# Eight of sixteen gates moved to the seven-product form, the filler's pace in the attention halved, and the first half of the heads' results fetched inside the last pair of heads

## The chip, the cores and the metric

The kernel runs on one core of one Trainium2 chip. The core has five engines that run their own instruction streams side by side: TensorE (PE, matmuls; PEld is its weight load), VectorE (DVE), ScalarE (ACT), GpSimd (POOL) and SyncE (SP, used here only to issue DMAs). An engine takes its instructions in the order in which they were put down when the program was built; where one waits on a semaphore, all behind it on that engine wait too. The metric is the device time of one execution in microseconds (us); lower is better. The reference time of the kernel before is the median of three runs.

## The reference

One decoder block on x of 1024 tokens by 1024 channels, float32, one layer. The part that matters here is the token mixer:

```python
proj = xn @ w_in                      # xn: RMSNorm(x); 1024 x 5136
(sb_q, sb_k, sb_v, g_q, g_k, g_v, g_r, g_a, gate_sb, gate_gla) = split(proj)
o_sb  = stick_breaking_attention(...) # 8 heads x 64, causal, blocks of 128
o_gla = gla_chunked(...)              # 4 heads, dk 64, dv 128
y = (sigmoid(gate_sb  + b_gate[0]) * (o_sb  @ w_branch_sb)
   + sigmoid(gate_gla + b_gate[1]) * (o_gla @ w_branch_gla))
h = x + y @ w_out
h = h + conv_ffn(rms_norm(h))         # gated MLP, d_ff 2816, causal conv of width 3
```

The two merge gates together are 2048 columns of `w_in`, that is 16 blocks of 128 channels; a "gate" below is one such block for all 1024 tokens. Gates 0 to 7 belong to the stick-breaking branch and 8 to 15 to the GLA branch.

## The kernel before, in words

All tensors stay float32 in effect: each operand is split into a high part (rounded to the matmul's float32 form) and the low remainder, and a product is three matmuls (high x high, high x low, low x high). `split` (L119, L110) does this with a cast on ACT and a subtraction on DVE; `add`, `sub`, `mul` (L116, L110, L113) are DVE operations; `mac` (L196) is the loop of matmuls, of 128x128 weights against 512 columns.

The stages in order of time:

1. **Norm and values** (0 to about 114 us): RMSNorm of x, transposes into four quarters `xq["11"]` to `xq["22"]` (token half, channel half), the value projections (L367), and the sums of quarters `s1` to `s4` for the seven-product form.
2. **Seven-product projections** (about 114 to 311 us), `fast` (called at L618): one job takes two blocks of 128 columns of `w_in` against all tokens. Written directly that is 2 blocks x 2 token halves x 8 channel blocks x 3 = 96 matmuls; with seven products of half-size operands in place of eight (Winograd's form of Strassen) it is 7 x 4 x 3 = 84, at the price of additions on DVE: four for the weights' sums, seven splits and seven to combine the products. `project_pairs` (L454) lists the jobs: two for the GLA queries and keys, four for the attention's queries and keys, two for the output gate `gr`, and `N_GATES`/2 = 2 for the first four merge gates. `keep` (L520) finishes a job: for a gate, a sigmoid of 128x1024 on ACT and a DMA to `gate_d` from ACT's queue.
3. **Attention** (about 311 to 540 us), `attend` (L705). Four pairs of heads (`j`); in each, four pairs of query blocks (`tp`); in each, both heads (`e`). A query block `i` sees `i+1` key blocks, in chunks of up to four blocks. For a chunk, `weigh` (L665) makes the logits (2 matmuls, L672), a sigmoid on ACT (L674) and a scan on DVE (L677, or L679 where a chunk goes on from another); `turn_weights` (L683) transposes the result block by block on PE (L686) and splits it; `gather` (L689) multiplies it with the values (L695), adds a bias on ACT (L701) and writes the head's result, as a high and a low part, to `osb_d` from SP's queue (L703). Up to six chunks, or twelve blocks, are under way between `weigh` and `turn_weights` (`AHEAD`, `BLOCKS`). Over all heads this is 8 x 36 = 288 blocks.
4. **Gates in between.** The other 12 gates are made directly by the generator `gates` (L539), 24 matmuls for each token half, cut in four steps of six. `attend` yields the number of blocks after each chunk, and the loop at L757 runs one gate step for each `FILL` = 3.6 blocks owed; six more steps come early (L742), and a sigmoid (L567) and a DMA follow every fourth step. Steps of the second token half need `xq["21"]`, which `whole21` (L605) fetches again from `x21_d` early in the attention and casts on ACT (L613). The first three gates do their second half last. What is left is run after the attention: four steps at L957, the rest at L969.
5. **Between attention and GLA** (about 540 to 565 us): loads for the GLA (L776 to L781), then the heads' results: for each token half `th` and each of four blocks `k`, two DMAs from `osb_d` (L964), one add and one split give `ob[th]`. Each DMA's target is a buffer of the pool `t2` (11 of them), each `ob[th]` takes two of the 16 buffers of pool `t8`.
6. **GLA with the first branch in between** (to about 620 us), then the second branch, the output projection, the FFN (L196 again as seven-product jobs, then L1155) and the final norm.

The order of instructions on each engine is set when the program is built, by a list scheduler that follows the order of the program's text as a priority; gate steps stand 25 places lower than their place in the text (`LATER`).

Of the kernel before, what the change touches and what calls it, by code (L numbers as in the profile page):

```python
# [17 lines left out]
P = 128  # L18
# [4 lines left out]
HALF = 512  # L23
SBH, SBD = 8, 64
# [10 lines left out]
C_GATE = 3088  # L35
T2 = 11
T4 = 14
FILL = 3.6
EACH = 0
LATER = 25  # L40
MORE = 1
# [11 lines left out]
GLA = 2, 3  # L53
PACES = 0, 0, 0, 1
EARLY = 6
N_GATES = 4
AT_END = 51
N_READY = 1
N_OPS = 11
# [6 lines left out]
def block_kernel(ctx: ExitStack, tc: tile.TileContext, x, norm_mix_g, w_in, b_gate, w_alpha_up, b_alpha,  # L66
                 gla_norm_g, w_branch_sb, w_branch_gla, w_out, norm_ffn_g, w_ffn_in, conv_w, conv_b,
                 w_ffn_out, norm_final_g, out):
    nc = tc.nc
# [7 lines left out]
    def nm(s):  # L77
        uid[0] += 1
        return f"{s}_{uid[0]}"
# [7 lines left out]
    def t8(dt=F32R):  # L87
        return sb.tile([P, 2 * D], dt, tag="t8", name=nm("t8"), bufs=16)

    def t4(dt=F32):  # L90
        return sb.tile([P, D], dt, tag="t4", name=nm("t4"), bufs=T4)

    def t2(dt=F32):
        return sb.tile([P, HALF], dt, tag="t2", name=nm("t2"), bufs=T2)

    def bank():
        return ps.tile([P, HALF], F32, tag="bank", name=nm("bank"), bufs=8)

    def dram(name, rows, cols):
        return dp.tile([rows, cols], F32, tag=name, name=name)  # L100

    def by(a, k):
        return a.rearrange("p (k c) -> p k c", k=k)

    def quarter():

        return [by(t8(), 4) for _ in range(2)]

    def sub(o, a, b):
        nc.vector.tensor_tensor(out=o, in0=a, in1=b, op=ALU.subtract)  # L110
# [4 lines left out]
    def add(o, a, b):  # L115
        nc.vector.tensor_tensor(out=o, in0=a, in1=b, op=ALU.add)  # L116

    def split(h, l, src):
        nc.scalar.copy(h, src)  # L119
        sub(l, src, h.bitcast(F32))  # L120
# [39 lines left out]
    osb_d = dram("osb_d", 2 * SBH * SBD, S)  # L160
# [4 lines left out]
    def fill(steps, n):  # L165
        for _ in range(n):
            next(steps, None)
# [286 lines left out]
    def project_pairs():  # L454
# [4 lines left out]
        for j in range(0, 4, 2):  # L459
            yield tuple((C_GR + n * P, gr_d, n * P) for n in (j, j + 1))  # L460
        for g in range(0, N_GATES, 2):
            yield tuple((C_GATE + n * P, gate_d, n * P) for n in (g, g + 1))
# [76 lines left out]
    def gates():  # L539
# [5 lines left out]

        gs = range(N_GATES, 2 * NK)
        order = [(g, (0,)) for g in gs[:N_HALVES]]
# [135 lines left out]
    def turn_weights(ke, nb, ah, al):  # L683
# [2 lines left out]
            nc.tensor.transpose(pt[:, b * P:(b + 1) * P], ke[:, b * P:(b + 1) * P], ident)  # L686
        split(ah, al, by(pt[:, 0:nb * P], nb))

    def gather(head, tp, ah, al):  # L689
        po = bank()  # L690
        nb = 2 * tp + 2
        for b in range(nb):
            c0 = 0 if b < nb - 1 else P
            for n, a in enumerate((ah, al)):
                nc.tensor.matmul(po[:, c0:2 * P], vt[b][:, head, :], a[b // 4][:, b % 4, c0:],  # L695
                                 start=(b == 0 and n == 0), stop=(b == nb - 1 and n == 1))
        o = t2()[:, 0:2 * P]
        for n in range(2):
            c = slice(n * P, (n + 1) * P)
            i = head * NT + 2 * tp + n  # L700
            nc.scalar.activation(o[:, c], po[:, c], AF.Identity, bias=vend[:, i:i + 1])  # L701
        for n, r in enumerate(HALVES):
            nc.sync.dma_start(osb_d[n * HALF + head * 64:n * HALF + (head + 1) * 64, tp * 2 * P:(tp + 1) * 2 * P], o[r])  # L703

    def attend():  # L705

# [42 lines left out]
        while todo:  # L749
            flush()  # L750
            while late:
                gather(*late.popleft())
            yield 2
# [3 lines left out]
    for w in attend():  # L757
        owed += w + EACH
        while owed >= FILL:
            owed -= FILL  # L760
            fill(gate_steps, 1)
# [11 lines left out]
    for p in range(2):  # L773
        rows = slice(p * P, (p + 1) * P)
        v, kt = by(t8(F32), 2), t4()
# [114 lines left out]
    def branch(b, o, w):  # L890

        def pieces(i):
            if i < NK:
                if i % 2 == 0:
                    raws.append(load(w[:, i * P:(i + 2) * P], 4))
                return piece(raws[-1][:, :, i % 2 * P:(i % 2 + 1) * P])

        raws = []
        nxt = pieces(0)
        yield  # L900
        for i in range(NK):
            wp, nxt = nxt, pieces(i + 1)
            for th in range(2):
                sg = t2()
                g = b * NK + i
                nc.sync.dma_start(sg, gate_d[g * P:(g + 1) * P, th * HALF:(th + 1) * HALF])
                if i % 4 == 0:
                    if b == 0:
                        yb[th, i // 4] = by(t8(F32), 4)
                    else:  # L910
                        yq[th, i // 4] = quarter()
                pt = bank()
                mac([a[:, 0:2] for a in wp], [a[:, 0:2] for a in o[th]], 2, pt, stop=False)
                yield
                mac([a[:, 2:4] for a in wp], [a[:, 2:4] for a in o[th]], 2, pt, start=False)
                y = yb[th, i // 4][:, i % 4]
                if b == 0:
                    mul(y, pt, sg)
                else:
                    mul(sg, pt, sg)  # L920
                    add(sg, sg, y)
                    split(*(a[:, i % 4] for a in yq[th, i // 4]), sg)
                yield
# [31 lines left out]
            fill(wsteps, paced[n] % PACES[n] == 0)  # L955

    fill(gate_steps, BEFORE)  # L957
    ob = []
    for th in range(2):
        ob.append(quarter())  # L960
        for k in range(4):
            halves = t2(), t2()
            for n, v in enumerate(halves):
                nc.sync.dma_start(v, osb_d[n * HALF + k * P:n * HALF + (k + 1) * P, th * HALF:(th + 1) * HALF])  # L964
            add(halves[0], *halves)
            split(*(a[:, k] for a in ob[th]), halves[0])
    first_branch = branch(0, ob, w_branch_sb)
    fill(first_branch, 1)
    fill(gate_steps, 128)  # L969
# [2 lines left out]
    n = 0  # L972
# [319 lines left out]
```

## Time and profile before

| | us |
|---|---|
| median of three runs | 1414.32 (1413.01 to 1415.31) |
| profiled execution, its own time | 1414.5 |
| its span in the trace | 1412.8 |
| PE busy | 1382.6 (98% of the span) |
| DVE busy | 1055.3 (75%) |
| ACT busy | 647.0 (46%) |
| POOL busy | 90.0 (6%) |

Busy time is the union of an engine's instructions in the trace. The end of a matmul is modelled and overlaps the next one's start, so "busy" on PE says that no gap was seen, not that matmuls followed each other at full rate; the rate is read from the distance between starts. The chain of waits names, for each piece of time, the work that the end of the execution hung on.

### The profile page before, as it was taken

Reading aid. Unit: us, or ns where it says so; the run is one execution under the profiler, and the core shown is the slowest. Engines: PE = TensorE matmul, PEld = TensorE weight load, DVE = VectorE, ACT = ScalarE, POOL = GpSimd, SP = SyncE. Lnnn points to the kernel's source line nnn. Section 1 sums busy time; section 2 is a strip of 40 time slices with the busy share of each in tenths; the row PEclk is TensorE's granted clock in tenths of the full one; section 3 lists DMA queues with packets and bytes.
Section 4 is the critical chain, followed back from the end, with each engine's and each line's share of the span. In section 5 each row is a group of like instructions: output and inputs, shape, how many; then the busy total and the mean of one; then the engine's idle time right before and its main releaser. Section 6 shows DMA issues by size and latency. Waiting matters only on the chain.

```text
span 1412.8 us, 18288 instructions
## 1 busy us (share of the span) xinstructions
PE 1382.6 (98%) x6577; PEld 1143.9 (81%) x6577; DVE 1055.3 (75%) x1618; ACT 647.0 (46%) x1246; POOL 90.0 (6%) x159
## 2 busy tenths in 40 slices
PE   7999999999999998999999999999999999999996
PEld 6788888887888887878888788888888888888885
DVE  6387776767887774738446988999888977896764
ACT  6234334647766563643234543333333334454653
POOL 0002122200000000300000000000000000000000
PEclk9999999999999999999999999999999999999999
DMA  6334345476644447465324434564554537953232
GB/s 249 129 109 137 108 153 186 137 207 197 164 117 112 124 157 252 170 226 176 120 90 134 111 98 149 188 208 146 175 179 149 171 106 269 324 159 99 98 110 90
DMA packets 163131, 221.84 MB, mean 157 GB/s; under 512 B 10729, under 2 KB 106027, under 8 KB 162528
## 3 DMA queue, kind: packets, MB, share of 16 engines
q1 hardware_dynamic: 142272, 157.56, 36.1%
q0 software_dynamic: 13472, 48.56, 9.2%
q10 hardware_dynamic: 7296, 14.55, 2.8%
q8 instruction: 52, 0.85, 0.2%
q14 instruction: 39, 0.32, 0.1%
HBM read 158.37 MB, written 62.26 MB: 156 GB/s over the span
## 4 chain that ended last, share of the span: by engine, by line
PE 92%; DVE 3%; DMA 2%; ACT 1%; issue 0%; SPq 0%; DVEq 0%; ACTq 0%
PE bank L196 56%; PE bank L1155 15%; PE bank L367 6%; PE bank L1022 5%; PE bank L695 2%; PE bank L672 2%; PE bank L686 2%; DVE t L110 2%; DMA t<-osb_d 1%; PE bank L320 1%; DMA t<-x_d 1%; DVE t L116 1%; PE bank L427 1%; PE bank L826 1%; ACT t L119 0%
## 5 line engine op out<-in xcount | busy, mean ns | idle before, releaser
L196 PE MATMUL bank<-t,t 128*128 128x512 f32 x3648 | 869.3, 394 | 5.7 <-DVE t L110 5.2
L196 PEld LDWEIGHTS bank<-t,t 128*128 128x128 f32 x3648 | 681.6, 188 | 153.2 <-DVE t L110 7.1
L110 DVE TENSOR_TENSOR t<-t,t 128x512 fp32r<-128x512 f32 (+2 forms) x651 | 432.0, 698 | 89.7 <-ACT t L119 82.7
L119 ACT CAST t<-t 128x512 fp32r<-128x512 f32 x537 | 311.3, 620 | 313.5 <-DVE t L110 68.7
L116 DVE TENSOR_TENSOR t<-bank,t 128x512 f32<-128x512 f32 x252 | 170.2, 686 | 99.3 <-PE bank L196 58.3
L1155 PE MATMUL bank<-t,t 128*128 128x512 f32 x924 | 209.6, 390 | 0.0
L1155 PEld LDWEIGHTS bank<-t,t 128*128 128x128 f32 x924 | 173.5, 188 | 36.0
L110 DVE TENSOR_TENSOR t<-bank,t 128x512 fp32r<-128x512 f32 (+4 forms) x128 | 72.3, 580 | 38.6 <-ACT t L119 37.8
L110 DVE TENSOR_TENSOR t<-t 128x512 f32<-128x512 f32 (+1 forms) x124 | 88.9, 725 | 6.2 <-DMA t<-in_w_ffn_in_dram 4.1
L367 PE MATMUL bank<-t,t 128*128 128x512 f32 x384 | 91.1, 396 | 0.0
L116 DVE TENSOR_TENSOR t<-t,t 128x512 f32<-128x512 f32 x115 | 75.7, 689 | 19.9 <-ACT t L486 15.6
L1022 PE MATMUL bank<-t,t 128*128 128x512 f32 x384 | 88.9, 391 | 0.0
L1053 ACT ACTIVATE t<-t,vcol 128x1024 f32<-128x1024 f32 x22 | 27.4, 1244 | 126.8 <-DVE t L116 126.8
L367 PEld LDWEIGHTS bank<-t,t 128*128 128x128 f32 x384 | 72.2, 190 | 15.4 <-DVE t L110 0.4
L1022 PEld LDWEIGHTS bank<-t,t 128*128 128x128 f32 x384 | 71.7, 188 | 14.6
L119 ACT CAST t<-bank 128x512 fp32r<-128x512 f32 (+3 forms) x124 | 61.7, 510 | 38.4 <-PE bank L320 19.2
L1055 DVE SCALAR_TENSOR_TENSOR t<-t,vcol,t 128x1023 f32<-128x1023 f32 (+1 forms) x44 | 56.3, 1279 | 14.1 <-ACT t L1053 13.9
L677 DVE TENSOR_TENSOR_SCAN t<-t,t 128x128 f32<-128x128 f32 (+1 forms) x64 | 51.6, 816 | 20.2 <-ACT t L674 19.8
L672 PE MATMUL bank<-t,t 128*128 128x128 f32 (+3 forms) x192 | 55.0, 366 | 0.3 <-DVE t L110 0.3
L686 PE MATMUL bank<-ident,t 128*128 128x128 f32 x288 | 53.9, 274 | 0.1
L674 ACT ACTIVATE t<-bank 128x128 f32<-128x128 f32 (+3 forms) x96 | 45.8, 502 | 7.1 <-PE bank L672 6.8
L679 DVE TENSOR_TENSOR_SCAN t<-t,t,zero 128x512 f32<-128x512 f32 x32 | 41.0, 1281 | 9.8 <-ACT t L674 8.8
(133 smaller groups left out, 743.9 us busy)
## 6 DMA issues: line engine op xcount, KB each, us to landing
t<-in_w_ffn_in_dram SPq DMA_DIRECT2D x50, 512.0 KB, 4.3
t<-in_w_in_dram SPq DMA_DIRECT2D x43, 512.0 KB, 5.3
act_d<-t POOLq DMA_DIRECT2D x22, 512.0 KB, 6.2
t<-in_w_ffn_out_dram SPq DMA_DIRECT2D x22, 512.0 KB, 5.8
wsum_d<-t POOLq DMA_DIRECT2D x22, 512.0 KB, 4.5
t<-act_d SPq DMA_DIRECT2D x22, 512.0 KB, 5.8
t<-wsum_d SPq DMA_DIRECT2D x44, 256.0 KB, 3.2
t<-sqk_d SPq DMA_DIRECT2D x40, 256.0 KB, 4.2
```

The costliest lines, as they stand in the source:

```text
L110: nc.vector.tensor_tensor(out=o, in0=a, in1=b, op=ALU.subtract)
L116: nc.vector.tensor_tensor(out=o, in0=a, in1=b, op=ALU.add)
L119: nc.scalar.copy(h, src)
L196: nc.tensor.matmul(pt, a[:, kk], b[:, kk], start=start and kk == 0 and m == 0, stop=stop and kk == k - 1 and m == 2)
L367: nc.tensor.matmul(pt, a[:, k % 4, t], b, start=k == 0 and m == 0, stop=k == NK - 1 and m == 2)
L672: nc.tensor.matmul(z[:, 0:w], q[:, a, e, ts_], kk[:, e, b0 * P:b1 * P], start=a == 0, stop=a == 1)
L674: nc.scalar.activation(ke[:, 0:w], z[:, 0:w], AF.Sigmoid, scale=-SBD ** -0.5)
L677: nc.vector.tensor_tensor_scan(out=kr, data0=kr, data1=above[:, 0:w], initial=1.0, op0=ALU.mult, op1=ALU.max)
L686: nc.tensor.transpose(pt[:, b * P:(b + 1) * P], ke[:, b * P:(b + 1) * P], ident)
L1022: nc.tensor.matmul(pt, a[:, k % 4, t], b, start=(k == 0 and m == 0), stop=(k == NK - 1 and m == 2))
L1055: nc.vector.scalar_tensor_tensor(out=cv[:, i:], in0=av[:, :S - i], scalar=col(V_CW, (2 - i) * NF + f), in1=cv[:, i:], op0=ALU.mult, op1=AL ...
L1155: nc.tensor.matmul(pts[m][i], a[:, t], b, start=(k == 0 and x_ == 0), stop=(k == NH - 1 and x_ == 2))
```

## The change

Three edits. `N_GATES` goes from 4 to 8, so that two more jobs of the seven-product stage make gates 4 to 7, and `gates` makes 8 gates (8 to 15) and not 12. `FILL` goes from 3.6 to 6, so that a gate step is run for every six blocks of the attention. And the fetch of the heads' results becomes a function that `gather` calls for the last head: after the second of its four pairs of query blocks for the first token half, after the fourth for the second half. In the text of the program the second call now stands ahead of the loads for the GLA; before, both halves came behind them.

```diff
-FILL = 3.6
+FILL = 6
-N_GATES = 4
+N_GATES = 8
+    ob = []
+
+    def fetch_heads(th):
+
+        ob.append(quarter())
+        for k in range(4):
+            halves = t2(), t2()
+            for n, v in enumerate(halves):
+                nc.sync.dma_start(v, osb_d[n * HALF + k * P:n * HALF + (k + 1) * P, th * HALF:(th + 1) * HALF])
+            add(halves[0], *halves)
+            split(*(a[:, k] for a in ob[th]), halves[0])
+
     def gather(head, tp, ah, al):
...
             nc.sync.dma_start(osb_d[n * HALF + head * 64:n * HALF + (head + 1) * 64, tp * 2 * P:(tp + 1) * 2 * P], o[r])
+        if head == SBH - 1 and tp % 2:
+            fetch_heads(tp // 2)
...
     fill(gate_steps, BEFORE)
-    ob = []
-    for th in range(2):
-        ob.append(quarter())
-        for k in range(4):
-            halves = t2(), t2()
-            for n, v in enumerate(halves):
-                nc.sync.dma_start(v, osb_d[n * HALF + k * P:n * HALF + (k + 1) * P, th * HALF:(th + 1) * HALF])
-            add(halves[0], *halves)
-            split(*(a[:, k] for a in ob[th]), halves[0])
     first_branch = branch(0, ob, w_branch_sb)
```

## The prediction

> **What bounds the kernel now.** I read the page's chain first: its shares by engine, then by line.
>
> ```profile
> PE 92%; DVE 3%; DMA 2%; ACT 1%; issue 0%; SPq 0%; DVEq 0%; ACTq 0%
> ```
>
> The end hangs on TensorE for 92% of the span, so a matmul saved is worth its time wherever the other engines keep up, and a pause of PE costs its length. Next comes the chain in order of time, for the price of a matmul, and the windows (columns: window, its length, busy time and count on PE, PEld, DVE, ACT, POOL, granted clock, DMA share, GB/s; the second answer is L196 alone, PE and PEld).
>
> ```profile
> 253.41 38.31 PE bank L196 x168
> 292.15 19.09 PE bank L196 x84
> ```
>
> ```profile
> 253.40:293.20 39.80, 39.80 (x179) 32.97 (x179) 33.22 (x52) 26.01 (x38) 7.77 (x14) 1.00 0.48 150
> 758.00:797.00 39.00, 38.15 (x179) 30.76 (x178) 38.49 (x64) 25.38 (x48) 1.59 (x3) 1.00 0.57 162
> 797.00:1193.00 396.00, 396.00 (x1749) 328.01 (x1748) 344.78 (x500) 145.65 (x217) 22.85 (x43) 1.00 0.47 158
> ...
> 311.50:538.70 227.20, 225.60 (x1329) 194.04 (x1326) 170.03 (x240) 145.20 (x326) 0.00 (x0) 1.00 0.50 145
> ...
> 311.50:538.70 227.20, 146.56 (x525) 95.37 (x525) 1.00 0.50 145
> ```
>
> The first chain row is the eighth and ninth of the ten seven-product jobs, the ninth being the first of the two gate jobs; the second row is the last job, also gates. Two jobs of 84 matmuls take 38.31 us, 0.228 us a matmul, with no gap, while DVE is busy for 33.22 of 39.80 us. The attention runs from 311.5 to 538.7: 227.2 us, PE without gaps but for 1.6 us, DVE at 170.03/227.2 = 75%. Of its PE time the 525 matmuls of L196 take 525 x 0.228 = 119.7 us (all 12 gates are 12 x 48 = 576; 51 come later); the attention's own logits, transposes and gathers have the other 107.5 us. So here the direct gates are more than half of what PE does, and hide everything else.
>
> Then the joint of attention and GLA, by the timeline of PE (start, busy time; in brackets the idle time before and its releaser), the windows there, and the waits (total, times, longest).
>
> ```profile
> 552.86 1.97 PE L196 MATMUL bank<-t,t 128*128 128x512 f32 x7
> 556.45 0.96 PE L196 MATMUL bank<-t,t 128*128 128x512 f32 x3 [1.62 <-DVE t L110]
> ...
> 562.18 1.65 PE L196 MATMUL bank<-t,t 128*128 128x512 f32 x5 [2.78 <-DVE t L110]
> 564.23 3.54 PE L196 MATMUL bank<-t,t 128*128 128x512 f32 x9 [0.40 <-ACT t L119]
> ```
>
> ```profile
> 560.00:565.00 5.00, 2.42 (x7) 1.51 (x8) 4.10 (x8) 1.76 (x3) 0.40 (x1) 0.84 1.04 381
> 565.00:570.00 5.00, 5.00 (x30) 3.87 (x29) 4.68 (x13) 1.82 (x4) 2.03 (x6) 0.82 1.00 350
> ```
>
> ```profile
> DVE t L116 <- DMA t<-osb_d: 3.7, 2, 2.1
> ACT t L613 <- DMA t<-x_d: 2.8, 2, 1.9
> ```
>
> PE stands for 1.62 + 2.78 + 0.40 = 4.80 us: the first branch's matmuls wait for the split of the fetched heads' results (L110 and L119 behind the add L116). Then nine matmuls take 3.54 us where 9 x 0.228 = 2.05 would do, another 1.5, at a granted clock of 0.84 and 0.82. The joint costs 6.3 us.
>
> **The change part by part.**
>
> *Jobs added.* Two more jobs are 168 matmuls: **+38.3 us** by the row of x168. What they bring to the other engines is what the present gate jobs bring, and that row shows it hidden: DVE 33.22, ACT 26.01 of 39.80. Their weight loads on SP and gate DMAs on ACT's queue are those of jobs 9 and 10 again (DMA share 0.48). If that cover were gone PE would wait for DVE; at 83% it is far from it. Bounds: 38 to 39.
>
> *Direct gates removed.* Four gates are 4 x 48 = 192 matmuls, 192 x 0.228 = **-43.8 us**, all from the attention if the pacing lets go as many as the work shrinks. It does: 288 blocks / 3.6 = 80 steps before, 288 / 6 = 48 after, 32 fewer, and four gates are 32 steps (two halves of four). The remainder run after the attention stays about as it is (51 matmuls), and covers the joint as now. Both parts together are 24 matmuls less, -5.5 us. PE alone would then finish the attention in 227.2 - 43.8 = 183.4 us.
>
> *What is late next in the attention.* VectorE. Its 170.03 us do not shrink with the gates:
>
> ```profile
> L679 DVE TENSOR_TENSOR_SCAN t<-t,t,zero 128x512 f32<-128x512 f32 x32 | 41.0, 1281 | 9.8 <-ACT t L674 8.8
> L110 DVE TENSOR_TENSOR t<-bank,t 128x512 fp32r<-128x512 f32 x45 | 30.3, 674 | 1.8 <-ACT t L119 1.8
> L110 DVE TENSOR_TENSOR t<-t,t 128x512 fp32r<-128x512 f32 x34 | 21.8, 679 | 3.7 <-ACT t L119 3.6
> ```
>
> Scans and the splits of transposes belong to the blocks (groups of 312 to 530 us, columns: busy, mean ns, idle before). Only the split of gate weights goes: each of the 15 visits to a gate splits two halves of 128x512; eight gates have 11 visits, so 4 x 2 x 0.679 = 5.4 us go, and the moved fetch adds four adds and four subtractions, 8 x 0.68 = 5.4. DVE keeps 170 us, which in 183.4 is 93%, up from 75%. It cannot use all of it: at the start and the end it waits for work, whatever the fill.
>
> ```profile
> 313.49 1.25 DVE L677 TENSOR_TENSOR_SCAN t<-t,t 128x128 f32<-128x128 f32 x2 [1.32 <-ACT t L674]
> ...
> 319.82 1.29 DVE L110 TENSOR_TENSOR t<-t,t 128x512 fp32r<-128x512 f32 x2 [2.98 <-ACT t L119]
> ...
> 534.80 1.89 DVE L110 TENSOR_TENSOR t<-bank,t 128x512 fp32r<-128x512 f32 x3 [4.54 <-ACT t L119]
> ```
>
> That is 1.3 + 3.0 + 4.5 = 8.8 us, and 2 us more after its last piece at 536.7. 170 of 183.4 - 10.8 = 172.6 us is 98%. So PE and DVE become bounds together, which no row of the attention shows yet. Two rows bound it: 758 to 797 us has DVE at 38.49 of 39.00 with PE idle 0.85 us (2.2%, or 4 us in 183); 797 to 1193 us has DVE at 344.78/396 = 87% and PE without a gap. If the attention ran DVE at no more than those 87%, it would last 170 / 0.87 = 195.4 us, 12 above PE's own time. Bounds of this stall: 0 to 12; I take **+3**, near the first row, since the 758 to 797 us are the only ones that show both full. It should sit where the keys and queries of the next pair are split, where DVE already has most to do, against the next 20 us without them:
>
> ```profile
> 450.00:470.00 20.00, 20.00 (x116) 16.96 (x116) 17.47 (x24) 13.28 (x31) 0.00 (x0) 1.00 0.26 74
> 470.00:490.00 20.00, 20.00 (x126) 17.80 (x125) 13.73 (x20) 9.77 (x24) 0.00 (x0) 1.00 0.48 145
> ```
>
> In 20 x 183.4/227.2 = 16.1 us the first needs 17.5 us of DVE: some 1 us over, at each of three such places.
>
> *The start.* ACT waits 2.8 us in all for the reload of x's quarter (L613), with casts and sigmoids of the chunks queued behind it and DVE behind those; PE, full of gate steps, loses little:
>
> ```profile
> 346.45 0.39 PE L695 MATMUL bank<-t,t 128*128 128x256 f32 x1 [1.17 <-DVE t L110]
> ```
>
> With 0.6 of the gate steps PE has less to bridge it: between 0 and 2.8 us more; I take **+1**.
>
> *The fetch inside the last pair.* Eight loads of 256 KB on SP, four adds, four casts on ACT, four subtractions, at about five sixths of the attention. The adds wait for loads, and behind them on DVE are scans and splits; behind the loads on SP are the write-outs of other heads' results, gate weights and the GLA's loads. The present fetch made DVE wait 3.7 us (row above), among crowded DMAs. The pool `t2` is shared with the chunks, so the look-ahead shrinks while it runs. Bounds 0 to 4; I take **+1.5**.
>
> *The joint.* When the last results are written, only half the fetch is left, and the matmuls of the first token half no longer wait. DVE's timeline has the adds of the fetch, first and last:
>
> ```profile
> 548.22 0.69 DVE L116 TENSOR_TENSOR t<-t,t 128x512 f32<-128x512 f32 x1
> ...
> 562.85 0.67 DVE L116 TENSOR_TENSOR t<-t,t 128x512 f32<-128x512 f32 x1
> ```
>
> Both halves end with the split behind 562.85, when PE goes on for good; the first ends where PE goes on at 556.45. Half a fetch is thus done near 556.4, and PE, fed without a gap to 554.8 (row of 552.86) and then by matmuls of the first token half, has next to nothing to wait for. The 4.80 us of idle go, and with them the slow clock, 6.3 in all. Against it the GLA's loads now stand behind the second fetch in the text. I take **-5.3**, between 0 and -6.3.
>
> The Trainium skill, "TensorE: Matmul & The Clock Gate" (Part 1, The HAM clock gate), says that the array's clock falls to half after an idle window of about 3.4 us and is given back after a busy one of that length. The two rows at 560 to 570 us, 0.84 and 0.82 in the mean behind gaps of 1.62 and 2.78 us, agree with a clock lost for part of that time, though no single gap was that long. The rule speaks against thinner filling: gaps in the attention would cost more than their length (a rival below).
>
> **Sum.** +38.3 - 43.8 + 3 + 1 + 1.5 - 5.3 = -5.3 us. The profiled execution took 1414.5 us, its span 1412.8; 1414.5 - 5.3 = 1409.2, and since the median 1414.32 is 0.2 lower: **1409.0**.
>
> **The rivals.**
>
> *A, the forecast:* attention 186 to 191 us, joint mostly closed; 1406 to 1412. Chance 0.40.
>
> *B, all of it lands:* look-ahead of twelve blocks absorbs DVE's peaks, the stalls are nil: -5.5 - 6.3 = -11.8, 1402.5. For it: DVE's total still fits, 98% of what it can use. Against: only 39 us of trace show such packing. 0.15.
>
> ```profile
> L674 ACT ACTIVATE t<-bank 128x512 f32<-128x512 f32 x48 | 29.0, 606 | 6.7 <-PE bank L672 6.6
> L119 ACT CAST t<-bank 128x512 fp32r<-128x512 f32 x45 | 26.8, 597 | 10.0 <-PE bank L686 9.9
> ```
>
> *C, slower: VectorE's chain takes over the attention.* Scan, cast and split wait in turn, and PE, in order, stands at each transpose whose scan is late. It decides from a use of DVE below 87%: then the 195.4 us are past and the stall of 12 eats the whole 11.8. At 83%, what the gate jobs show beside a bound PE (33.22/39.80), it is 170/0.83 = 205 us, 21.4 over PE's time: 1414.3 + 21.4 - 11.8 = 1424. For it: twelve blocks of look-ahead are 227.2/288 x 12 = 9.5 us now and 7.6 after, against a chain of some 4.4 us (sigmoid 0.61 and cast 0.60 by the rows above, two scans of 1.28, split 0.67) plus transposes and queues. Against: DVE waits today mostly because nothing is there to do. 0.18.
>
> *D, the joint stays:* the early fetch finds no buffers (`t8` is nearly full: four quarters, the values and the last pair take 15 of 16) and is done late, or the GLA's loads now collide with it and PE waits for those. Then the 5.3 are not had: 1414.3. 0.20.
>
> *E, the clock:* gaps in the attention bring the slow clock. Ten us at 0.83 lose 1.7 us; at the start and the three crowded places that is 4 x 1.7 = 6.8 on top of the forecast: 1415.8. The skill's page on the clock gate, named above, would have it so for gaps beyond 3.4 us; the attention's rows now show 1.00 throughout. 0.07.
>
> **How the numbers follow.** Noise and small differences: 0.2% is 2.8 us, about what a measurement of this kernel tells from no change, so faster is below 1411.5 and slower above 1417.1. Faster: B 0.15, most of A 0.37, 0.03 of D: 0.55. Same: 0.03 of A, 0.15 of D, 0.03 of C, 0.04 of E: 0.25. Slower: 0.15 of C, 0.02 of D, 0.03 of E: 0.20. The range leaves out the lowest of B and the upper half of C: 1402 to 1420.
>
> **What would show it.** The seven-product stage ends near 311.5 + 38.3 = 349.8 us. The attention then lasts 186 to 191 us with DVE around 90%; B shows 183 and no gaps on PE, C 196 or more with PE idle before L686 and L695, released by DVE. At the joint the waits of PE for L110 are gone and the granted clock stays at 1.00; D shows gaps there of 4 us or more. Everything from the second branch on keeps its length. The forecast is wrong if the attention's gaps sum to over 9 us, or if the 38.3 us of the two jobs come with gaps of their own.

## The result and the profile after

The kernel after takes 1427.85 us (median of 5 runs, 1426.43 to 1429.32), the kernel before on the same chip 1414.41 (5 runs): a ratio of 1.0097 with a 95% interval of 1.0087 to 1.0108. It is **slower**, by about 13.4 us. The forecast was 1409.0, faster; the range ended at 1420. The profiled execution took 1427.94 us, 13.4 more than that of before, so it can be taken apart stage by stage.

Three marks cut the span: the first matmul of the attention (the small transposes of L651), the last bias of the attention on ACT (L701 before, L713 after), and the stretch of 250 matmuls of L196 in the chain of waits, from which on both kernels run alike.

| | attention starts | last bias | x250 starts | attention lasts | joint lasts |
|---|---|---|---|---|---|
| before | 311.18 | 538.88 | 620.32 | 227.7 | 81.4 |
| after | 349.11 | 543.40 | 633.58 | 194.3 | 90.2 |
| difference | +37.9 | +4.5 | +13.3 | -33.4 | +8.8 |

(The joint, from the last bias to the x250, has the rest of the gates, the fetch, the GLA and the first branch.) So the two added jobs cost what was forecast, the attention gave back 33.4 us instead of 38.3, and the joint, which was to get 5.3 us shorter, got 8.8 us longer. The joint holds 14 of the 19 us between forecast and result. Each row is cut from one profiled execution.

The windows of after (columns as in the prediction: window, length, PE, PEld, DVE, ACT, POOL, granted clock, DMA share, GB/s):

```profile
520.00:525.00 5.00, 2.88 (x14) 2.06 (x13) 4.55 (x7) 4.23 (x11) 0.00 (x0) 1.00 0.45 152
525.00:530.00 5.00, 3.78 (x17) 2.93 (x17) 5.00 (x7) 3.27 (x6) 0.00 (x0) 0.60 0.74 181
530.00:535.00 5.00, 5.00 (x26) 4.47 (x25) 5.00 (x7) 2.65 (x6) 0.00 (x0) 0.72 0.03 8
...
543.20:570.00 26.80, 13.58 (x58) 10.39 (x58) 7.92 (x14) 7.15 (x13) 0.36 (x1) 0.82 1.02 363
560.00:570.00 10.00, 0.76 (x2) 0.54 (x3) 0.79 (x2) 1.14 (x2) 0.00 (x0) 0.51 1.06 395
570.00:580.00 10.00, 10.00 (x38) 8.23 (x37) 5.28 (x14) 2.28 (x4) 2.28 (x5) 0.81 0.67 225
```

Two places stand out. In the attention PE has gaps between 520 and 530 us, and then runs at a granted clock of 0.60 and 0.72. In the joint every engine is nearly idle between 560 and 570 us, and only the DMA engines are full. The timeline of PE has four gaps in these two places (start, busy; in brackets the idle time before and what ended it):

```profile
524.85 0.63 PE L686 MATMUL bank<-ident,t 128*128 128x128 f32 x4 [2.12 <-DVE t L679]
527.16 1.09 PE L686 MATMUL bank<-ident,t 128*128 128x128 f32 x4 [1.22 <-ACT t L674]
557.52 0.67 PE L803 MATMUL bank<-t,t 128*128 128x256 f32 x2 [2.17 <-issue]
569.24 2.93 PE L196 MATMUL bank<-t,t 128*128 128x512 f32 x6 [11.05 <-ACT t L119]
```

Before, PE stood for 4.80 us in the joint; now 2.17 + 11.05 = 13.22 (two gaps near the joint's end, 2.7 us together, are the same in both kernels and left out). These 8.4 us more are the 8.8 of the table but for 0.4. The gap of 11.05 names a cast on ACT, but the chain in order of time says what the cast waited for:

```profile
545.82 4.46 DMA t<-osb_d
...
552.36 0.70 DVE t L116
...
553.14 6.46 DMA gate_d<-t
...
559.62 8.93 DMA t<-in_w_branch_sb_dram
...
568.57 0.63 ACT t L119
...
569.24 2.93 PE bank L196 x6
...
633.58 57.52 PE bank L196 x250
```

The fetched results are no longer late: their last add is done at 553.1, where before it was at 563.5. Late are the first weights of the branch, `in_w_branch_sb`, which are issued at 559.62 and take 8.93 us to land. Why so late is seen in SP's own timeline, after:

```profile
545.19 4.20 SPq L697 DMA_DIRECT2D t<-osb_d  x8
549.44 0.45 SPq L792 DMA_DIRECT2D t<-gv_d  x1
551.80 0.32 SPq L794 DMA_DIRECT2D t<-qd_d  x1
...
557.50 0.32 SPq L795 DMA_DIRECT2D t<-ki_d  x1
559.62 0.38 SPq L172 DMA_DIRECT2D t<-in_w_branch_sb_dram  x1
```

and before, in the same stretch (the second fence is the answer for the line of the gv loads: count, duration in ns, first and last start):

```profile
540.73 0.53 SPq L172 DMA_DIRECT2D t<-in_w_branch_sb_dram  x1
541.31 14.76 SPq L964 DMA_DIRECT2D t<-osb_d  x16
```

```profile
L778 SPq DMA_DIRECT2D t<-gv_d x2: 377/482/587, 472.3 to 512.9; - x2
...
DMA to landing us min/median/max: 5.6/5.9/6.3
```

Before, the GLA's six loads (gv, qd, ki; 4 MB in all) were issued between 472 and 514 us, beside the attention, and the branch weights at 540.73, ahead of the whole fetch. After, all of them stand behind the second half of the fetch, between 549.4 and 559.6. By the window's 363 GB/s the 4.19 MB of the GLA's loads are 11.6 us of traffic (an estimate), now in front of the branch weights and at a time when nothing covers them. Issuing takes SP some 0.4 us each; for 8.0 of the 10.2 us from 549.44 to 559.62 it waits for earlier DMAs to land: 3.7 us for the fetch, 2.5 for the first gv load, and at the end 1.8 for the write of a gate (the `gate_d` row of the chain), with which the branch weights have no data in common. Why SP waits for such a write is said at e16.

The Trainium skill, "DMA: Bandwidth & Descriptors" ("Specifications"), gives 435 GB/s as the ceiling of the fabric. The windows here, 363 and 395 GB/s at a DMA share above 1, stand at 83% and 91% of it; by page and trace the loads are near the bandwidth, and it is their order that can be mended.

### The profile page after: what moved, and what is told of

Read it like the earlier page. It is cut to its first block, busy times and chain, and to the rows that moved or that the text cites. A ratio compares the mean times of both kernels' runs of the same rounds, so it can differ in the third digit from the quotient of the medians.

```text
span 1426.2 us, 18278 instructions
## 1 busy us (share of the span) xinstructions
PE 1383.0 (97%) x6553; PEld 1141.9 (80%) x6553; DVE 1070.3 (75%) x1646; ACT 649.5 (46%) x1250; POOL 90.0 (6%) x159
## 4 chain that ended last, share of the span: by engine, by line
PE 65%; DVE 3%; DMA 2%; ACT 1%; issue 0%; SPq 0%; ACTq 0%; DVEq 0%
PE bank L196 37%; PE bank L1160 15%; PE bank L1027 5%; PE bank L707 2%; DVE t L110 2%; PE bank L686 2%; PE bank L672 2%; DVE t L116 1%; DMA t<-osb_d 1%; DMA t<-in_w_branch_sb_dram 1%; PE bank L840 1%; PE bank L803 0%; DMA gate_d<-t 0%; PE bank L875 0%; PE bank L827 0%
## 5 line engine op out<-in xcount | busy, mean ns | idle before, releaser
L196 PE MATMUL bank<-t,t 128*128 128x512 f32 x3624 | 862.1, 394 | 11.9 <-ACT t L119 11.1
L196 PEld LDWEIGHTS bank<-t,t 128*128 128x128 f32 x3624 | 677.8, 188 | 157.2 <-ACT t L119 12.2
L110 DVE TENSOR_TENSOR t<-t,t 128x512 fp32r<-128x512 f32 (+1 forms) x661 | 437.6, 694 | 96.1 <-ACT t L119 88.9
L119 ACT CAST t<-t 128x512 fp32r<-128x512 f32 x543 | 315.1, 620 | 328.4 <-DVE t L110 73.2
L116 DVE TENSOR_TENSOR t<-bank,t 128x512 f32<-128x512 f32 x266 | 179.0, 684 | 111.4 <-PE bank L196 72.0
L1160 PEld LDWEIGHTS bank<-t,t 128*128 128x128 f32 x924 | 173.5, 188 | 36.0
L110 DVE TENSOR_TENSOR t<-t 128x512 f32<-128x512 f32 (+1 forms) x128 | 91.0, 719 | 10.9 <-ACT t L601 7.0
L110 DVE TENSOR_TENSOR t<-bank,t 128x512 fp32r<-128x512 f32 (+4 forms) x128 | 71.6, 575 | 24.5 <-ACT t L119 24.3
L367 PEld LDWEIGHTS bank<-t,t 128*128 128x128 f32 x384 | 72.3, 190 | 15.4 <-DVE t L110 0.4
L1027 PEld LDWEIGHTS bank<-t,t 128*128 128x128 f32 x384 | 71.7, 188 | 14.7
L1060 DVE SCALAR_TENSOR_TENSOR t<-t,vcol,t 128x1023 f32<-128x1023 f32 (+1 forms) x44 | 56.2, 1278 | 14.1 <-ACT t L1058 13.9
L677 DVE TENSOR_TENSOR_SCAN t<-t,t 128x128 f32<-128x128 f32 (+1 forms) x64 | 51.3, 810 | 11.1 <-ACT t L674 10.8
L707 PE MATMUL bank<-t,t 128*128 128x256 f32 (+1 forms) x320 | 50.5, 280 | 1.8 <-DVE t L110 1.8
L707 PEld LDWEIGHTS bank<-t,t 128*128 128x128 f32 x320 | 46.1, 192 | 4.7 <-DVE t L110 2.7
```

The lines of the kernel that those rows point to most:

```text
L196: nc.tensor.matmul(pt, a[:, kk], b[:, kk], start=start and kk == 0 and m == 0, stop=stop and kk == k - 1 and m == 2)
L367: nc.tensor.matmul(pt, a[:, k % 4, t], b, start=k == 0 and m == 0, stop=k == NK - 1 and m == 2)
L677: nc.vector.tensor_tensor_scan(out=kr, data0=kr, data1=above[:, 0:w], initial=1.0, op0=ALU.mult, op1=ALU.max)
L1027: nc.tensor.matmul(pt, a[:, k % 4, t], b, start=(k == 0 and m == 0), stop=(k == NK - 1 and m == 2))
L1060: nc.vector.scalar_tensor_tensor(out=cv[:, i:], in0=av[:, :S - i], scalar=col(V_CW, (2 - i) * NF + f), in1=cv[:, i:], op0=ALU.mult, op1=AL ...
L1160: nc.tensor.matmul(pts[m][i], a[:, t], b, start=(k == 0 and x_ == 0), stop=(k == NH - 1 and x_ == 2))
```

## The experiments

All kernels against the kernel before; each ratio is taken against executions of the kernel before in the same series, whose median lay between 1413.51 and 1414.83. "Weights" is the time from the last bias of the attention to the issue of the first branch weights (negative where it comes earlier); attention and joint are cut as above, in us, from one profiled execution each. Executions of one kernel can lie 6 us apart (before, beside e5 to e8: 1411.27 to 1417.65), and the attention lasts 188.3 us in e1 and 190.6 in e5, where the program's text for it is the same; a difference of 2 us between two cuts shows little by itself.

| run | attention | weights | joint | median | ratio (95%) |
|---|---|---|---|---|---|
| before | 227.7 | 1.9 | 81.4 | 1414.41 | |
| after | 194.3 | 16.2 | 90.2 | 1427.85 | 1.0097 (1.0087 to 1.0108) |
| e1_gates_only | 188.3 | 12.7 | 84.6 | 1416.48 | 1.0018 (1.0008 to 1.0028) |
| e2_fetch_only | 229.3 | 17.0 | 90.5 | 1424.77 | 1.0076 (1.0060 to 1.0091) |
| e3_late_half | 195.0 | 9.7 | 82.8 | 1422.56 | 1.0059 (1.0044 to 1.0074) |
| e4_branch_first | 193.8 | -3.4 | 95.5 | 1434.62 | 1.0143 (1.0128 to 1.0158) |
| e5_gates_preload | 190.6 | 3.0 | 76.5 | 1407.82 | 0.9950 (0.9933 to 0.9966) |
| e6_gla_first | 196.5 | 5.3 | 77.3 | 1417.75 | 1.0026 (1.0015 to 1.0036) |
| e7_spread8 | 192.1 | 4.1 | 77.0 | 1414.60 | 0.9998 (0.9988 to 1.0008) |
| e8_spread4 | 231.9 | 1.8 | 72.8 | 1411.55 | 0.9978 (0.9968 to 0.9987) |
| e9_pool_adds | 195.4 | 17.3 | 90.0 | 1429.55 | 1.0111 (1.0096 to 1.0126) |
| e10_gates6 | 215.0 | 1.8 | 79.2 | 1419.31 | 1.0046 (1.0028 to 1.0064) |
| e11_gates12 | 176.2 | 1.8 | 80.3 | 1439.03 | 1.0177 (1.0155 to 1.0200) |
| e12_pool_subs | 197.4 | 3.0 | 76.0 | 1419.75 | 1.0044 (1.0027 to 1.0061) |
| e13_stagger | 191.1 | 16.1 | 90.2 | 1425.60 | 1.0082 (1.0069 to 1.0096) |
| e14_stagger8 | 191.2 | 2.9 | 74.4 | 1410.71 | 0.9977 (0.9968 to 0.9986) |
| e15_stagger4 | 229.5 | 1.8 | 73.9 | 1408.62 | 0.9963 (0.9950 to 0.9977) |
| e16_before_preload | 226.5 | 1.8 | 80.3 | 1414.83 | 1.0005 (0.9996 to 1.0014) |

The theory after the result: the moved fetch pushes other loads behind it, and PE waits for those (rival D's second half, with a price that D had not given it). Its rival: the gates' thinner filling leaves PE without cover at the joint.

**The two parts alone.** e1 is the kernel before with the two constants changed; e2 is the kernel after with the two constants changed back.

```diff
-FILL = 3.6
+FILL = 6
-N_GATES = 4
+N_GATES = 8
```

> N_GATES 8 and FILL 6 alone, the fetch of the heads' results back at its old place behind the GLA's loads. Theory 1 (the early fetch pushes the GLA's loads and the first branch weights behind it): the attention loses the 3.3 us of gaps and the slow clock of the fetch and lasts about 188 us, the gap of PE at the joint falls from 13.2 us to about 5 to 8; 1414 to 1418 us. Theory 2 (the thinner filling leaves the joint without cover, whatever the fetch does): the joint keeps a gap of 11 us or more; 1422 to 1428 us.

```diff
-FILL = 6
+FILL = 3.6
-N_GATES = 8
+N_GATES = 4
```

> The fetch inside the last pair alone, with 4 gates in the seven-product form and FILL 3.6. Theory 1: the joint has the gap of 11 to 13 us that the changed kernel has; 1420 to 1426 us. Theory 2: the joint's 4.8 us of gaps go; 1406 to 1411 us.

e2 takes 10.8 of the 13.4 us of loss: with the old gates the moved fetch alone makes the joint 9.1 us longer. Its attention is only 1.6 us longer than before. e1 shows the other part as it was forecast in the attention, and a loss at the joint even there:

```profile
349.40:537.10 187.70, 184.44 (x1133) 157.56 (x1133) 161.88 (x232) 134.74 (x311) 0.00 (x0) 1.00 0.54 153
```

```profile
557.13 3.02 PE L196 MATMUL bank<-t,t 128*128 128x512 f32 x6 [7.75 <-ACT t L119]
```

```profile
538.87 10.66 SPq L964 DMA_DIRECT2D t<-osb_d  x16
549.76 0.38 SPq L172 DMA_DIRECT2D t<-in_w_branch_sb_dram  x1
```

The attention is 39.4 us shorter than before, at a full clock. But the branch weights, which stand behind the fetch in the program's text and which the scheduler's order had put ahead of it before, now come behind all 16 loads of the fetch, and PE stands 7.75 us. The chain in front of that gap names not the load itself but the last add of the fetch:

```profile
555.30 0.61 DVE t L116
555.94 1.15 ACT t L119 x2
```

Of these two casts the first is of the last fetched result and the second of the weights, which stands behind it on ACT; the weights land some 6 us after their issue, as that add ends. So e1 does not tell the late load from the late cast. The rival theory falls in its simple form: the same number of gate matmuls is left for the joint (576 - 526 = 50 before, 384 - 334 = 50 in e1), so it is the place of the weights, not the cover.

**The load put back in its place.** e5 is e1 with the first branch weights loaded ahead of the fetch in the text (the branch then takes that buffer as its first).

```diff
+    early_raws = [load(w_branch_sb[:, 0:2 * P], 4)]
     ob = []
     for th in range(2):
...
-        raws = []
+        raws = early_raws if b == 0 else []
```

> e1 (eight gates in seven-product form, FILL 6, fetch at its old place) with the first load of the branch weights put ahead of the fetch in the text. If that load, which e1 issues last, at 549.8 us, is what its gap of 7.75 us waits for: the gap falls to the 5 us of the kernel before, 1412 to 1414.5 us. If the split of the heads' results ends the gap anyway: within 1 us of e1, 1415.5 to 1417.5 us.

```profile
549.08 0.73 PE L196 MATMUL bank<-t,t 128*128 128x512 f32 x2 [1.63 <-ACT t L119]
```

```profile
542.65 0.38 SPq L172 DMA_DIRECT2D t<-in_w_branch_sb_dram  x1
```

One line moved, the load and with it its cast (548.41 on ACT, ahead of most of the fetch), takes the gap from 7.75 to 1.63 us and the joint from 84.6 to 76.5. That is better than either theory had it (a gap of 5 us, 1412 to 1414.5); 1407.82 us is the lowest median of the study, 0.5% (0.34 to 0.67) below before. Its profiled execution was its slowest of four (1410.66), so its attention of 190.6 should be read beside e1's 188.3.

**The same load alone.** e16 puts it there in the kernel before, with four gates.

> The kernel before, with its four gates and its fetch where it was, and only the load of the first branch weights put ahead of the fetch, as in e5. If the gain of e5 comes from the eight gates and that load only gives back what the thinner filling had cost the joint, nothing is gained here, since the kernel before issues that load at 540.7 us, ahead of the fetch, as it is: 1413-1415. If the load's place is the gain by itself, 1406-1410, and the eight gates are worth nothing.

No difference, as expected of a load that is already in its place (1.8 us behind the last bias, against 1.9). So the gain of e5 needs the gates. Part of it is the gates' own (e1: +37.6 in the jobs, -39.4 in the attention); the other part is 4.9 us of the joint, and the waits of SP's queue (total, times, longest) show a reason. In e16:

```profile
SPq L965 <- DMA gate_d<-t: 4.3, 1, 4.3
```

and in e5:

```profile
SPq L906 <- DMA gate_d<-t: 2.2, 1, 2.2
```

With four gates a load of the fetch (L965) stands 4.3 us behind the write of a finished gate, with which it has no data in common (3.7 us in the kernel before): the program counts the DMAs of SP's and ACT's queues on eight semaphores in turn, and a DMA waits for the earlier one on its own. (The fetch and the gates' results also share the pool `t2`, so a common buffer is not ruled out here; the branch weights of after go to `t4` and waited for a gate's write all the same.) With eight gates the count falls otherwise, and the one that waits for that write is the later reload of a gate (L906). That this is all of the 4.9 us was not tried.

**The order mended with the early fetch kept.** e3 leaves the second half of the fetch behind the GLA's loads; e4 puts the branch weights ahead of the second half; e6 puts the GLA's loads ahead of both.

```diff
-        if head == SBH - 1 and tp % 2:
+        if head == SBH - 1 and tp == 1:
             fetch_heads(tp // 2)
...
     fill(gate_steps, BEFORE)
+    fetch_heads(1)
```

> The changed kernel with the fetch of the second token half put back behind the GLA's loads in the text; the first half stays in the last pair. Theory 1: the GLA's loads are issued before the end of the attention and the joint's gap falls from 13.2 to 5 us or less; 1416 to 1421 us. Theory 2: no change, 1426 to 1429 us.

```diff
         if head == SBH - 1 and tp % 2:
+            if tp == 3:
+                early_raws.append(load(w_branch_sb[:, 0:2 * P], 4))
             fetch_heads(tp // 2)
```

> The changed kernel with the load of the first branch weights put ahead of the second fetch, so that it is not behind the GLA's loads on SP; all else stays. If that load is what PE waits for at the joint: the gap of 11.05 us goes or shrinks below 4; 1416 to 1420 us. If the GLA's 4 MB themselves are what is late: the gap moves to the GLA's first matmuls and stays at 8 us or more; 1424 to 1428 us.

```diff
         if head == SBH - 1 and tp % 2:
+            if tp == 1:
+                gla_loads()
             fetch_heads(tp // 2)
```

> The changed kernel with the GLA's loads put ahead of the first early fetch in the text. If their place behind the fetch makes the joint long: the GLA's loads are issued before 525 us, the gap of 13 us falls to 3 to 7, and what is left over the kernel before is the 6 us that the fetch costs inside the attention; 1416 to 1421 us. If buffers hold those loads back whatever the order: 1425 to 1429 us.

e3 and e6 shorten the joint to 82.8 and 77.3 us as the weights come earlier, and leave the attention long. e6 ends in its range; e3's gaps, 2.95 + 1.80 us, are as expected, its time is 1.6 us above its range. e4 was a miss: its joint is the longest of all, although its branch weights come 3.4 us ahead of the last bias.

```profile
568.68 0.80 PE L196 MATMUL bank<-t,t 128*128 128x512 f32 x1 [19.54 <-ACT t L119]
```

```profile
568.01 1.66 ACT L119 CAST t<-t 128x512 fp32r<-128x512 f32 x3 [11.44 <-DMA t<-in_w_in_dram]
```

```profile
539.37 0.53 SPq L172 DMA_DIRECT2D t<-in_w_branch_sb_dram  x1
...
557.15 0.38 SPq L172 DMA_DIRECT2D t<-in_w_in_dram  x1
```

PE now stands 19.54 us (PE's, ACT's and SP's timelines), and ACT's casts name the load: the last weights of a gate, `in_w_in`, issued only at 557.15, behind the GLA's. They come from the same pool of buffers (`t4`) as the branch weights; the load that was put ahead has, as I read it, taken the buffer that the gate's would have had; no run tries this. A load's place may also be the buffer that it takes.

e7 and e8 place everything by what is needed first: the GLA's loads in the last head's gather `tp` 1, the first half of the fetch in the next, then the branch weights, then the second half where it was before; with eight gates and with four.

```diff
-        if head == SBH - 1 and tp % 2:
-            fetch_heads(tp // 2)
+        if head == SBH - 1:
+            if tp == 1:
+                gla_loads()
+            if tp == 2:
+                fetch_heads(0)
...
     fill(gate_steps, BEFORE)
+    early_raws = [load(w_branch_sb[:, 0:2 * P], 4)]
+    fetch_heads(1)
```

> Eight gates, FILL 6, the GLA's large loads in the text at the second query pair of the last head, the first half's fetch after its third query pair (when VectorE runs out of chunks), then the first branch weights, then the second half's fetch. If the cost of the change is the order of the loads and the fetch's place among the chunks, not the fetch as such: no fetch cost in the attention (under 2 us), joint gap under 3 us; 1407 to 1412 us. If half a fetch inside the attention costs its 6 us wherever it stands: 1414 to 1418 us.

> The same order of loads as e7 with four gates in the seven-product form and FILL 3.6. If the order of the loads is the cause: 1407 to 1411 us, some 5 us below the kernel before, by its joint gap alone. If not: 1414 or more.

With four gates this is 0.2% faster than before, the joint being 72.8 us, the shortest of all (13 gate matmuls, 3.0 us, of it having moved into the attention): the early half does what it was to do, once it stands behind what is needed earlier. With eight it is no gain over before. PE still stands 4.27 us in the joint, for the last weights of a gate, as in e4 (ACT's timeline):

```profile
548.66 1.14 ACT L119 CAST t<-t 128x512 fp32r<-128x512 f32 x2 [6.04 <-DMA t<-in_w_in_dram]
```

The median of e7 is 6.8 us behind e5's, but the two profiled executions are only 1.3 us apart (1411.93 and 1410.66), so most of that difference cannot be read from these traces.

**What the early fetch costs inside the attention.** After's attention is 6.0 us longer than e1's (194.3 against 188.3), with the same 334 gate matmuls in it. The gaps above are 2.12 + 1.22 = 3.3 us, and PE is busy 2.8 us longer, in windows where the clock is 0.60 and 0.72. With four gates the same fetch opens gaps of 0.39 + 1.06 us there (e2) and costs 1.6 us in all: it is the thinner filling that lets the wait through. The chain of after in front of the first gap (start, us, what):

```profile
517.27 4.92 DMA t<-osb_d
...
522.82 0.68 DVE t L110
523.50 1.21 DVE t L679
...
524.85 0.64 PE bank L686 x4
```

A load of the fetch is on its way until 522.19, an add and a split on DVE stand in order for it, and behind them the scan (L679) that the next transposes need. e9 moves the adds from DVE to POOL; e13 keeps them on DVE, but loads each block one gather before its add is asked for.

```diff
-            add(halves[0], *halves)
+            nc.gpsimd.tensor_tensor(out=halves[0], in0=halves[0], in1=halves[1], op=ALU.add)
```

> The changed kernel with the eight adds of the early fetch on GpSimd, which is idle in the attention, so that VectorE no longer stands in order before an add that waits for a load. If that wait is what opens the 3.3 us of gaps near 523 us and brings the slow clock behind them (some 3 us more): 1421 to 1425 us. If the casts and splits behind the adds, or the shared buffers, do it: 1426.5 to 1429 us.

In e13, `load_head` has the two loads of a block and `join_head` its add and split; m counts the gathers of the last two heads.

```diff
+    def staggered(m):
+        if 1 <= m <= 4:
+            join_head(0, m - 1)
+        if 0 <= m <= 3:
+            load_head(0, m)
...
-        if head == SBH - 1 and tp % 2:
-            fetch_heads(tp // 2)
+        if head >= SBH - 2:
+            staggered(2 * tp + head - SBH - 1)
+            if head == SBH - 1 and tp == 3:
+                fetch_heads(1)
```

> The kernel after with each block of the early fetch loaded one gather before its sum and split are asked for, so that no engine stands in order for an osb load; the second half and GLA's loads stay where the change put them. If the wait in order is what costs the attention its 6 us, the attention goes from 194.0 to 188-190 us and the time to 1421-1424. If it is the fetch's own work or its buffers, the attention stays at 193-195 and the time at 1427-1429. The joint stays near 90 us in either case.

e9 gains nothing (1429.55, above both ranges): ACT, in order, now waits for POOL (first row, ACT's timeline), and DVE's scans beside POOL's adds take nearly twice as long (DVE's timeline; they are 1.28 and 1.21 us in the mean elsewhere).

```profile
520.96 0.62 ACT L119 CAST t<-t 128x512 fp32r<-128x512 f32 x1 [3.75 <-POOL t L698]
```

```profile
523.72 2.28 DVE L679 TENSOR_TENSOR_SCAN t<-t,t,zero 128x512 f32<-128x512 f32 x1
525.92 2.23 DVE L677 TENSOR_TENSOR_SCAN t<-t,t 128x512 f32<-128x512 f32 x1
```

e13 closes the gaps. The attention falls to 191.1 us, with six gate matmuls more in it than after's (340; 6 x 0.228 = 1.4 us), so 189.7 for the same work, and its windows show no gap at the old place and a full clock:

```profile
520.00:525.00 5.00, 5.00 (x29) 4.23 (x28) 4.78 (x7) 2.55 (x7) 0.00 (x0) 1.00 0.47 124
525.00:530.00 5.00, 4.95 (x31) 3.93 (x30) 5.00 (x7) 4.66 (x11) 0.00 (x0) 1.00 0.51 167
530.00:535.00 5.00, 5.00 (x37) 4.47 (x35) 4.41 (x7) 2.85 (x8) 0.00 (x0) 1.00 0.39 77
```

By these traces, of the 6.0 us some 4.6 were the gaps and the clock lost behind them, and 1.4 the fetch's own work. The split is rough: the total, 1425.6, is 1.6 us above the range expected for this cause and only 2.3 below after's, with overlapping intervals. And e13 does two things, for it also spreads the eight loads over four gathers; that the stand in order alone made the gaps is the likelier reading, not shown. e14 and e15 do the same to e7 and e8.

> e7_spread8 (eight gates, GLA's loads and the first branch weights ahead of the late half of the fetch) with the early half staggered in the same way. If the wait in order is the cause, the attention falls from 192.0 to 187-189 us with the joint at 77, and the time is 1407-1411. If not, it stays at 1413-1415.

> The same with four gates as seven-product jobs as in the kernel before. If the wait in order is the cause, 1406-1410 against 1411.6 of e8_spread4; if not, 1411-1413.

The times come as expected, 1414.60 to 1410.71 and 1411.55 to 1408.62 (the intervals of e7 and e14 lie apart, those of e8 and e15 overlap), but not from where they were expected. e14's attention is 191.2 us, not 187 to 189; with its gate matmuls counted (338, and 346 in e7) it is no shorter than e7's, and the same holds for e15 (529, and 539 in e8). There was no stand near 523 us left to remove: e7's attention, less 12 matmuls or 2.7 us, is 1.1 us over e1's. What falls is PE's idle time in the joint, from 4.27 to 1.41 us in e14 and by e8's gap of 1.46 us in e15; why was not tried. e15, four gates with the staggered early half, comes to within a microsecond of e5; the two intervals overlap, and which is the better isn't settled. With eight gates the same order (e14) is not shown to be better than with four.

**How many gates, and is DVE the next bound?** e10 and e11 are e5 with six gates (`FILL` 4.4) and with twelve (`FILL` 16); e12 is e5 with the subtractions of the keys' and queries' splits on POOL (L603, shown, and L591 in the same way).

```diff
-FILL = 6
+FILL = 4.4
-N_GATES = 8
+N_GATES = 6
```

> e5 with six gates in the seven-product form and FILL 4.4: 12 matmuls (2.7 us) less than the kernel before in place of 24, with ten direct gates to fill the attention. If e5 still loses 4 to 6 us in the attention because VectorE is nearly full there, this loses 1 to 3 and comes out level: 1406.5 to 1410 us. If those stalls have nothing to do with the filling: 1410 to 1412 us.

```diff
-FILL = 6
+FILL = 16
-N_GATES = 8
+N_GATES = 12
```

> e5 with twelve gates in the seven-product form and FILL 16. TensorE alone would save 24 more matmuls: 1402 us. If VectorE bounds the attention from there on, it cannot fall much below its own 157 us of work and some 11 us in which it has nothing to do, against 144 us of TensorE: 1424 to 1433 us.

```diff
-        sub(q[:, 1], q[:, 1].bitcast(F32), q[:, 0].bitcast(F32))
+        nc.gpsimd.tensor_tensor(out=q[:, 1], in0=q[:, 1].bitcast(F32), in1=q[:, 0].bitcast(F32), op=ALU.subtract)
```

> e5 with the subtractions that split keys and queries (about 15 us of VectorE in the attention) on GpSimd. If VectorE's load is what leaves gaps on TensorE in e5's attention: 2 to 4 us less, 1403.5 to 1406 us. If it is not: 1406.5 to 1409 us. If GpSimd is too slow for the next pair's keys: above 1410.

With twelve gates PE waits for DVE, as the trace of e11 says:

```profile
387.00:563.10 176.10, 155.08 (x958) 131.44 (x958) 155.93 (x225) 123.58 (x296) 0.00 (x0) 0.95 0.50 139
```

PE has work for 155 of 176 us, and its waits there are nearly all for scans and splits (L679, L110). DVE is busy for 155.93/176.10 = 89%; most of the rest it waits for ACT's casts (8.2 us) and sigmoids (7.6 us), so the bound is the chain through DVE and ACT rather than DVE's work alone. The loss was larger than expected; the clock, 0.95 in the mean, has a part in it. With six gates the result was worse than with four or eight, which no theory had. The attention is as long as its matmuls say (444 in place of 334: 110 x 0.228 = 25.1 us more than e5's 190.6, 215.7 against 215.0 measured). But the pacing of 4.4 leaves only 36 gate matmuls for the joint where the others have 50, and PE stands there for 1.13 + 0.47 + 3.54 us, against 1.63 in e5: a joint of 79.2 in place of 76.5, with 3.2 us of gate work less in it. The rival theory, the cover, would fit, but the chain in front of the last of these gaps goes through something else:

```profile
552.49 6.19 DMA gate_d<-t
559.06 3.57 DMA t<-osb_d
562.73 0.69 DVE t L116
563.42 0.61 DVE t L110
```

A load of the fetch stands 6.3 us behind the write of a gate, the wait of e16 once more, and the results behind it come late. Fewer matmuls are left to cover that wait; the two were not tried apart.

e12 took work from DVE and made it busier, and PE's gaps in the attention grew from 5.0 to 9.6 us. The group of the long scans (columns: busy, mean ns, idle before), first e5, then e12:

```profile
L679 DVE TENSOR_TENSOR_SCAN t<-t,t,zero 128x512 f32<-128x512 f32 x32 | 40.9, 1278 | 2.3 <-ACT t L674 1.2
```

```profile
L679 DVE TENSOR_TENSOR_SCAN t<-t,t,zero 128x512 f32<-128x512 f32 x32 | 46.4, 1451 | 5.2 <-ACT t L674 3.4 <-ACT t L119 0.5 <-DVE t L677 0.5
```

## Why the prediction was wrong

**Jobs added, +38.3: right.** 37.9 measured, without gaps of their own.

**Direct gates removed, -43.8, with +3 for DVE and +1 at the start: right.** That is -39.8; e1, which has nothing else in its attention, measured -39.4. DVE was not at 98% of what it can use, though: without the fetch its work shrank to 161.88 us in e1's window, 8 less than the 170.03 of before, where the sum had 5.4 leave. At 161.88/187.70 = 86% PE lost only some 4 us. That is just past rival C's point (87%), for which it gave a stall of 12. C's mechanism (scan, cast and split wait in turn) is real, and e11 shows it at twelve gates.

**The fetch inside the last pair, +1.5 (bounds 0 to 4): the term was mis-sized, and its bound too low.** It was 6.0 (e1 against after). With four gates it is 1.6 (before against e2), as taken; with the filler's pace halved, the wait for one late load comes through to PE, and PE then gets the slow clock. The prediction named both ("The adds wait for loads, and behind them on DVE are scans and splits", and rival E) and priced neither into this term, nor that its own thinner filling would lay the wait open.

**The joint, -5.3 (between 0 and -6.3): this is the step that failed.** It measured +8.8. The prediction was right that the fetch's results would come early enough: they did, by some 10 us. It said that "PE ... has next to nothing to wait for", having looked only at the wait that goes. It had noted that the GLA's loads "now stand behind the second fetch in the text" and priced that at nothing: six loads with 4 MB went from 472 to 514 us to 549 to 558, and the branch weights behind them from 540.7 to 559.6. The upper bound of the step, 0, was no bound. Rival D had the mechanism (it named the GLA's loads; the wait was for the branch weights behind them) and the wrong price: "the 5.3 are not had" was meant as its worst, where e2 shows that the displaced loads cost 9 us of their own.

That the two parts of the change could hurt each other was not seen either, in the attention (above) as at the joint. Even with the fetch left where it was, the new gates let the scheduler put the branch weights behind it (e1), at 3.2 us of the joint; that one line (e5) decides between 1416.5 and 1407.8.

The clock: rival E's mechanism (gaps bring the slow clock) was there. The granted clock of after is 0.76 in the mean of 525 to 527 us and 0.50 in that of 527 to 530, so it fell near 526 us (an estimate from these two): behind the gap of 2.12 us and 0.63 us of work, as the gap of 1.22 us began. The Trainium skill, "TensorE: Matmul & The Clock Gate" (Part 1, The HAM clock gate), would have it after some 3.4 us of idle; here it came after a gap of 2.12 us.

## What to carry to other kernels

When a load is moved up, list what it is now ahead of: in its queue, in its pool of buffers and on the semaphores it shares; what was issued early and covered may become the load that all wait for. A wait that goes at a joint is worth its length only up to the wait that is late next, so price that one from the trace. Loads whose result an in-order engine will use are better asked for one step before than in the same step (e13: the gaps went). A filler that is thinned lays open waits that it had covered: the same fetch cost the attention 1.6 us with four gates and 6.0 with eight.

## What the runs showed of the hardware that was not expected

- PE's granted clock was 0.60 in the mean of 525 to 530 us of after, behind a gap of only 2.12 us and beside one of 1.22, and was 1.00 again by 535 us.
- A two-input operation on POOL stretches DVE's scans beside it: 1.28 to 2.28 us for one scan (e9), 1278 to 1451 ns in the mean over 32 (e12). The Trainium skill, "SBUF — State Buffer" ("Who interferes with whom"), says that a DVE instruction with two inputs in SBUF contends with a GpSimd one that reads SBUF; the scans here have two, and that they are stretched agrees. Moving those subtractions off DVE left it busier (162.26 to 165.34 us in the attention).
- Crowded loads land later: among the fetch and the GLA's other loads, at 363 GB/s, the two gv loads took 8.0 and 10.7 us to land, against 5.6 and 6.3 beside the attention.
